# Local attention in blocks of 64 queries and 192 keys, and part of a gelu on GpSimd, in a Trainium2 decoder layer

## The chip, the core and the metric

The kernel runs on one core of a Trainium2 chip. Its engines each follow a fixed row of instructions of their own: TensorE (PE, with its weight loads shown as PEld), VectorE (DVE), ScalarE (ACT), GpSimd (POOL) and SyncE (SP), which issues most DMAs. An engine passes from one instruction to the next when the semaphores it waits for are reached, so an instruction that waits holds up all that stand behind it in the row of its engine. The metric is the device time of one execution in microseconds (us), median over runs; lower is better. One profiled execution gives the trace.

## The reference

One layer of a hybrid decoder on a prompt of 1024 tokens and eight single-token samples, width 1024, in fp32. Cut to what matters here:

```python
z = x @ w_in
xr, yr, q, k, v, xq, g = jnp.split(z, SPLIT_IDX, axis=-1)
xc, conv_new = causal_conv(xr, conv_buf, conv_w, conv_b)
hs, h_new = rg_lru(xc, h0, lru_wa, lru_ba, lru_wx, lru_bx, lru_lambda)   # h_t = a_t * h_(t-1) + u_t
a_out = hs * jax.nn.gelu(yr, approximate=True)        # branch a
s_out = swa_prompt(q, k, v, sinks)                    # branch s: 16 q heads, 4 kv heads of 64, window 128
c_out = mem_attn(xq, mem_k, mem_v)                    # branch c
merged = sum(gates[:, :, n] * (br @ w_branch[n]) for n, br in enumerate((a_out, s_out, c_out)))
h = layer_norm(ALPHA * x + merged @ w_out, ln1_g, ln1_b)
h = layer_norm(ALPHA * h + (jax.nn.silu(h @ w_gate) * (h @ w_up)) @ w_down, ln2_g, ln2_b)

# swa_prompt, per block of 128 queries: 256 keys, of which the band lets each query see 128
s = jnp.einsum('bnqkgd,bnmkd->bnkgqm', qb, kband) * scale
p = sink_softmax(jnp.where((m <= qi + 128) & (m > qi), s, -1e30), sinks)
o = jnp.einsum('bnkgqm,bnmkd->bnqkgd', p, vband)
```

## The kernel before

Every fp32 product is split in a high and a low part, and three matmuls (high by high, high by low, low by high) add up in one PSUM bank. ScalarE casts the high part and VectorE subtracts to get the low one (`split`). The stages follow one another: the projections (`project`), the attention to the memory, the local attention (`windows`), the rest of the branches, the output product and the feed-forward part. Names in the trace are those of the tiles.

*Projections.* 28 units of two column blocks of `w_in` (`UNITS`) go through seven steps each (`fast_step`, a Strassen scheme; 24 matmuls of 258 columns a step, in two halves p). The bank `ub` is built up in steps 0, 2, 4 and 6, and ScalarE copies it away after steps 0 and 2 (`p1s`, `u2s`), so step 4 has to wait for `u2s`; after step 6 `zb` is read from it. After each step, `pump` lets a side job go one stretch further. One kind of side job is `lru(m)` for m = 0 to 7: gates with a tanh, a square root, a scan along time on VectorE (`sq`), then the gelu of `yr`: a square, the product (g + 1) * yr, a tanh, once more (g + 1) * yr, and the product with the scan. `spill` writes q, k and xq, split in two, to DRAM (`scr_q`, ...).

*Windows.* For each of 4 kv heads and 8 blocks `b` of 128 queries: `win_scores` multiplies the four q heads of the group with 256 keys (128 in the first block). Queries and keys lie as high part over low part, 64 rows each, so two matmuls make one head's scores. A VectorE reduction adds the mask and finds the maximum, ScalarE takes the exponential with a running sum, and the four scalings by the reciprocal go to ScalarE (two), GpSimd and VectorE. `win_turn` transposes the probabilities by TensorE in two banks `bt` and splits them (`bph`, `bpl`); `win_values` multiplies them with `v` (bank `bo`). Values are stored as high and low parts side by side, so the two halves of the bank are added on the way out. Between blocks `fill(1)` puts one branch product of 24 matmuls (`bra`, `brc`: 8 tiles of weights, 3 matmuls each); `product` multiplies it by its gate and adds it into `M`. `windows` is a pipeline: scores of block b, a branch product, values of block b - 2, transposes of block b - 1.

What sets the order: a scheduler orders each engine's row when the kernel is built, by the program's order, dependences and its own estimates; `issue_after` pins an instruction behind another. `self.mark`, set in `mm3`, is such a pin: the values stand behind that matmul of the branch product.

## Time and profile before

| what | us |
|---|---|
| median of 3 runs | 1907.53 |
| lowest and highest | 1904.34 and 1908.17 |
| the profiled execution | 1903.72 |
| its span in the trace | 1902.0 |
| projections | 20 to 647 |
| attention to the memory | 647 to 816 |
| windows | 816 to 1012 |
| from there to the end | 1012 to 1902 |

The stages are read from the trace by their first and last matmuls, rounded. Rows of a timeline give start, duration, engine, line, operation and operands; x8 means that eight like rows are drawn together. Matmuls are pipelined: each is shown longer than the distance between two starts, and it is this distance that a matmul costs.

### The profile page before, as it was taken

How to read it: one execution, taken by the hardware profiler on the slowest of the kernel's cores; microseconds unless marked ns; L12 is line 12 of the kernel's file. 1: busy time of each engine (PE TensorE's matmuls, PEld its weight loads, DVE VectorE, ACT ScalarE, POOL GpSimd, SP SyncE). 2: the span in 40 equal slices, each digit the busy share in tenths (PEclk: the TensorE clock that was granted, in tenths of full speed). 3: DMA queues.
4: the chain of work that ended last, by engine and by line, in shares of the span. 5: the costliest groups of instructions: out<-in, count | busy, mean ns of one | idle time of the engine just before them, and what ended most of it. 6: DMA issues, size and time to landing. Idle time of an engine off the chain costs nothing.

```text
span 1902.0 us, 38091 instructions
## 1 busy us (share of the span) xinstructions
PE 1878.7 (99%) x14224; PEld 1860.1 (98%) x14224; DVE 1393.8 (73%) x2948; ACT 1018.4 (54%) x2187; POOL 288.4 (15%) x475
## 2 busy tenths in 40 slices
PE   8999999999999999999999999999999999999997
PEld 8999999999999999999999999999999999999997
DVE  8568877877887655469887667996766776686784
ACT  5455565555566555468775244653333333455574
POOL 1003000010000301012222111112111121222211
PEclk9999999999999999999999999999999999999999
DMA  7344444445345786577635563224353443586674
GB/s 233 111 147 167 142 165 152 141 158 198 120 163 184 256 268 197 161 191 216 166 110 164 178 213 112 90 91 162 132 166 123 144 156 128 185 295 219 202 230 133
DMA packets 177850, 321.98 MB, mean 169 GB/s; under 512 B 24577, under 2 KB 79953, under 8 KB 177665
## 3 DMA queue, kind: packets, MB, share of 16 engines
q1 hardware_dynamic: 157344, 258.90, 42.7%
q0 software_dynamic: 20320, 60.66, 9.6%
q8 instruction: 111, 1.82, 0.4%
q14 instruction: 75, 0.61, 0.1%
HBM read 234.50 MB, written 87.04 MB: 169 GB/s over the span
## 4 chain that ended last, share of the span: by engine, by line
PE 92%; ACT 3%; DVE 2%; DMA 1%; issue 1%; POOL 0%; SPq 0%; ACTq 0%; DVEq 0%; POOLq 0%
PE ub L338 5%; PE ub L337 5%; PE ub L339 5%; PE fb L1280 4%; PE fb L1281 4%; PE fb L1279 4%; PE dl L1567 3%; PE dl L1569 3%; PE dl L1568 3%; PE ud L338 3%; PE ud L339 3%; PE ud L337 3%; PE fd L1281 2%; PE fd L1280 2%; PE fd L1279 2%; PE op L134 2%
## 5 line engine op out<-in xcount | busy, mean ns | idle before, releaser
L641 ACT ACTIVATE bp<-bp,bst 128x257 f32<-128x257 f32 (+1 forms) x128 | 62.2, 488 | 30.0 <-DVE bst L637 29.9
L1343 POOL DMA_DIRECT2D scr_w<-dw x64 | 34.8, 544 | 271.0 <-DVE dw L1338 193.6
L97 ACT CAST u_1h<-us 128x512 fp32r<-128x512 f32 x48 | 29.8, 620 | 80.4 <-issue 45.2
L97 ACT CAST u_2h<-us 128x512 fp32r<-128x512 f32 x48 | 29.7, 619 | 78.6 <-PE fb L1280 37.8
L98 DVE TENSOR_TENSOR u_6l<-ur,u_6h 128x512 fp32r<-128x512 f32 x48 | 33.1, 690 | 46.7 <-PE fb L1281 28.4
L321 DVE TENSOR_TENSOR us<-ur,ur 128x512 f32<-128x512 f32 x96 | 65.9, 686 | 1.7
L321 DVE TENSOR_TENSOR us<-us,ur 128x512 f32<-128x512 f32 x96 | 65.9, 687 | 1.5
L134 PE MATMUL brs<-bsL,wbs_h 128*128 128x384 f32 (+2 forms) x192 | 61.3, 320 | 1.3 <-DVE bsL L98 1.3
L133 PE MATMUL brs<-bsH,wbs_h 128*128 128x258 f32 (+2 forms) x192 | 60.9, 320 | 0.3 <-ACT bsH L97 0.3
L135 PE MATMUL brs<-bsH,wbs_l 128*128 128x384 f32 (+2 forms) x192 | 61.1, 319 | 0.0
L833 POOL TENSOR_SCALAR tr<-th 128x1032 f32<-128x1032 f32 x8 | 12.0, 1496 | 315.1 <-DVE sq L832 110.9
L637 DVE CUSTOM_DVE_ANT_0 bp<-bs,mask,nsnk 128x256 f32<-128x256 f32 (+1 forms) x128 | 53.3, 459 | 4.9 <-PE bs L634 4.3
L97 ACT CAST u_4h<-us 128x512 fp32r<-128x512 f32 x48 | 29.8, 621 | 43.8 <-PE fb L1280 22.0
L97 ACT CAST u_0h<-ur 128x512 fp32r<-128x512 f32 x48 | 29.9, 622 | 42.7 <-PE ub L338 17.9
L648 POOL TENSOR_SCALAR bp<-bp,bst 128x256 f32<-128x256 f32 (+1 forms) x32 | 32.7, 1021 | 126.3 <-DVE bst L642 114.3
L97 ACT CAST u_3h<-ur 128x512 fp32r<-128x512 f32 x48 | 29.7, 620 | 41.0 <-PE ud L338 37.4
L98 DVE TENSOR_TENSOR u_5l<-us,u_5h 128x512 fp32r<-128x512 f32 x48 | 33.1, 689 | 21.9 <-PE ud L339 11.0
L805 POOL COPY pconv<-za 128x3 f32<-128x3 f32 x8 | 19.1, 2388 | 191.8 <-DVE za L369 189.2
L98 DVE TENSOR_TENSOR u_4l<-us,u_4h 128x512 fp32r<-128x512 f32 x48 | 33.0, 688 | 19.6 <-PE ub L339 10.9
L364 DVE TENSOR_TENSOR za<-uc,p1s 128x258 f32<-128x258 f32 x56 | 23.3, 421 | 31.6 <-PE uc L339 30.2
L1331 POOL DMA_DIRECT2D dw<-wdn x64 | 34.6, 540 | 77.8 <-DVE h_3l L98 45.7
L1307 ACT ACTIVATE ft<-za 128x516 f32<-128x516 f32 x40 | 25.3, 636 | 38.3 <-DVE za L1306 38.3
(1812 smaller groups left out, 8886.6 us busy)
## 6 DMA issues: line engine op xcount, KB each, us to landing
ur<-win SPq DMA_DIRECT2D x112, 256.0 KB, 2.9
ur<-wgu SPq DMA_DIRECT2D x80, 256.0 KB, 2.9
scr_f<-ft SPq DMA_DIRECT2D x40, 258.0 KB, 2.1
...
```

What stands on the lines that cost most here:

```text
L97: self.last_cast = ins = self.nc.scalar.copy(hi, src).ins
L98: self.last_sub = self.nc.vector.tensor_sub(lo, src, hi.bitcast(F32)).ins
L134: nc.tensor.matmul(ps, sh, ml, start=False, stop=False)
L135: self.last_mm = nc.tensor.matmul(ps, sl, mh, start=False, stop=closes and i == last).ins
L321: nc.vector.tensor_add(src, a, b)
L337: mm(sh[:, w], xh, start=opens and k == 0, stop=False)
L338: mm(sh[:, w], xl, start=False, stop=False)
L339: self.last_mm = mm(sl[:, w], xh, start=False, stop=k == 3).ins
L641: nc.scalar.activation(x, x, AF.Exp, bias=st[:, g:g + 1], scale=-1.0, accum_out=st[:, 4 + g:5 + g])
L1279: mm(sh[:, w], xh, start=opens and k == 0, stop=False)
L1280: mm(sh[:, w], xl, start=False, stop=False)
L1281: self.last_mm = mm(sl[:, w], xh, start=False, stop=k == 3).ins
```

## The change

In the windows, a block's 128 queries become two halves of 64. A tile of queries now holds 64 queries of two heads, and each half needs 192 keys only: eight matmuls of 192 columns for the scores, where there were eight of 256. The first and last 64 of the 256 keys concern one half each. They share a bank `be` of two transposes; the inner keys take four transposes in `bt`: six transposes instead of eight. `bt` is split as before (one cast, one subtraction of 512 columns), then the two ends are cast (both casts first) and subtracted, in tiles `bpe0` and `bpe1` that carry high part and low part over each other. The values are six matmuls of 256 columns instead of four of 512, and the end ones need `vd`, a copy of `v` with 64 rows twice, which eight more DMAs a kv head load. The reductions of the second pair of heads are pinned behind the last end subtraction. `scr_q` holds q in the new order, so that `spill` writes it in four DMAs with runs of 64 numbers instead of two with runs of 1024.

In the gelu, both products (g + 1) * yr leave VectorE for GpSimd, as an addition and a multiplication each. In `product`, the addition into `M` goes to GpSimd for the second branch (`c`), m below 6. The pin `mark` moves from the third to the last but one weight tile of a product.

```diff
+WK = 192
...
     def mm3(self, ps, terms, closes=True):
...
-            if i == 2:
+            if i == len(terms) - 2:
                 self.mark = self.last_mm
...
     def spill(self, z, m, name, scale):
...
-        nc.sync.dma_start(self.scr[name][:, m, 0, :], hp)
-        nc.sync.dma_start(self.scr[name][:, m, 1, :], zp)
+        for e, a in enumerate((hp, zp)):
+            if name == "q":
+                to = self.scr[name][:, m, e, :].rearrange("d (n u q) -> d u n q", u=2, q=64)
+                for u in range(2):
+                    nc.sync.dma_start(to[:, u], a[u * 64:(u + 1) * 64].rearrange("d (n q) -> d n q", q=64))
+            else:
+                nc.sync.dma_start(self.scr[name][:, m, e, :], a)
     def win_load(self, kv):
...
-        for g in range(4):
-            st = ph.tile([P, TP], F32R, tag="st", name=f"st{kv}_{g}", bufs=6)
+        q = [ph.tile([P, TP], F32R, tag="st", name=f"st{kv}_{n}", bufs=6) for n in range(4)]
+        for n in range(4):
             for e in range(2):
-                nc.sync.dma_start(st[e * 64:(e + 1) * 64].bitcast(F32), self.scr["q"][rows(g), 2 * kv + g // 2, e, :])
-            q.append(st)
+                nc.sync.dma_start(q[n][e * 64:(e + 1) * 64].bitcast(F32),
+                                  self.scr["q"][:, 2 * kv + n % 2, e, (n // 2) * TP:(n // 2 + 1) * TP])
         vs = ph.tile([P, 8, P], F32R, tag="vs", name=f"vs{kv}", bufs=2)
-        nc.sync.dma_start(vs.bitcast(F32), self.scr["v"][:, :, kv * P:(kv + 1) * P])
-        return ks, q, vs
+        v = self.scr["v"][:, :, kv * P:(kv + 1) * P]
+        nc.sync.dma_start(vs.bitcast(F32), v)
+        vd = [ph.tile([P, 4, 2, P], F32R, tag="vd", name=f"vd{kv}_{x}", bufs=2) for x in range(2)]
+        for x in range(2):
+            for r in range(2):
+                for e in range(2):
+                    nc.sync.dma_start(vd[x][e * 64:(e + 1) * 64, :, r, :].bitcast(F32),
+                                      v[r * 64:(r + 1) * 64, 4 * x:4 * x + 4])
+        return ks, q, (vs, vd)

     def win_scores(self, kv, ops, b):
...
-        p = self.ph.tile([P, 4, 257], F32, tag="p", name=f"bp{kv}_{b}", bufs=3)
-        pg = [p[:, g, :n] for g in range(4)]
-        nc.gpsimd.tensor_copy(p[:, :, n], snk)
+        p = self.ph.tile([P, 2, 2 * WK + 2], F32, tag="p", name=f"bp{kv}_{b}", bufs=3)
+        width = (WK, WK) if b else (64, P)
+        at = [(WK + 1 - width[0], WK + 1), (2 * WK + 1 - width[1], 2 * WK + 1)]
+        front, last = at[0][0] - 1, 2 * WK + 1
+        nc.gpsimd.tensor_copy(p[:, :, front:last + 1:last - front], snk.rearrange("p (r s) -> p r s", s=2))
+        pg = [p[:, pr, slice(*at[s])] for pr in range(2) for s in range(2)]
         for pr in range(2):
-            s = self.bank("s", f"bs{kv}_{b}_{pr}")
-            for u in range(2):
-                qq = q[2 * pr + u][:, b * P:(b + 1) * P]
-                o = s[:, u * 256:u * 256 + n]
-                nc.tensor.matmul(o, qq, ks[0][:, k0:k0 + n], start=True, stop=False)
-                nc.tensor.matmul(o, qq, ks[1][:, k0:k0 + n], start=False, stop=True)
-            for u in range(2):
-                g = 2 * pr + u
-                nc.vector.tensor_tensor_reduce(pg[g], s[:, u * 256:u * 256 + n], msk, 1.0, snk[:, g:g + 1],
-                                               ALU.add, ALU.min, st[:, g:g + 1])
+            ps = self.bank("s", f"bs{kv}_{b}_{pr}")
+            o = [ps[:, s * WK:s * WK + width[s]] for s in range(2)]
+            for s in range(2):
+                t0 = b * P + s * 64
+                qq = q[2 * (b // 4) + pr][:, 2 * t0 % TP:2 * t0 % TP + P]
+                kk = slice(t0 + 64 - width[s], t0 + 64)
+                nc.tensor.matmul(o[s], qq, ks[0][:, kk], start=True, stop=False)
+                nc.tensor.matmul(o[s], qq, ks[1][:, kk], start=False, stop=True)
+            for s in range(2):
+                g = 2 * pr + s
+                with self.tc.issue_after(self.last_sub) if pr else ExitStack():
+                    nc.vector.tensor_tensor_reduce(pg[g], o[s], self.mask[:, WK - width[s]:], 1.0, snk[:, g:g + 1],
+                                                   ALU.add, ALU.min, st[:, g:g + 1])
         for g in range(4):
-            x = p[:, g, :n + 1]
+            (k0, k1), s = at[g % 2], g % 2
+            x = p[:, g // 2, k0 - (s == 0):k1 + (s == 1)]
             nc.scalar.activation(x, x, AF.Exp, bias=st[:, g:g + 1], scale=-1.0, accum_out=st[:, 4 + g:5 + g])
...
-    def win_turn(self, kv, ops, b, pg):
+        return p
+
+    def win_turn(self, kv, ops, b, p):
         nc = self.nc
-        out = []
-        for kk in range(2 if b else 1):
-            pt = self.bank("t", f"bt{kv}_{b}_{kk}")
-            for g in range(4):
-                nc.tensor.transpose(pt[:, g * P:(g + 1) * P], pg[g][:, kk * P:(kk + 1) * P], self.ident)
-            hi = self.ph.tile([P, 512], F32R, tag="pt", name=f"bph{kv}_{b}_{kk}", bufs=4)
-            lo = self.ph.tile([P, 512], F32R, tag="pt", name=f"bpl{kv}_{b}_{kk}", bufs=4)
-            self.split(hi, lo, pt)
-            out.append((hi, lo))
-        return kv, ops[2], b, out
+        pt, pe = (self.bank("t", f"b{x}{kv}_{b}") for x in ("t", "e"))
+        nk = P if b else 64
+        for s in range(0 if b else 1, 2):
+            for pr in range(2):
+                o = s * 256 + pr * P
+                k0 = 2 * WK + 1 - P if s else 1
+                nc.tensor.transpose(pt[:, o:o + P], p[:, pr, k0:k0 + P], self.ident)
+        for pr in range(2):
+            nc.tensor.transpose(pe[:nk, pr * P:(pr + 1) * P], p[:, pr, P + 1:P + 1 + nk], self.ident)
+        hi = self.ph.tile([P, 512], F32R, tag="pt", name=f"bph{kv}_{b}", bufs=2)
+        lo = self.ph.tile([P, 512], F32R, tag="pt", name=f"bpl{kv}_{b}", bufs=2)
+        ends = [self.ph.tile([P, 256], F32R, tag=f"pe{s}", name=f"bpe{s}{kv}_{b}", bufs=1) for s in range(2)]
+        cols = slice(0 if b else 256, 512)
+        self.split(hi[:, cols], lo[:, cols], pt[:, cols])
+        own = [slice(s * 64, s * 64 + 64) for s in range(2)]
+        for s in range(2 if b else 1):
+            self.last_cast = nc.scalar.copy(ends[s][own[s]], pe[own[s], :256]).ins
+        for s in range(2 if b else 1):
+            self.last_sub = nc.vector.tensor_sub(ends[s][own[1 - s]], pe[own[s], :256],
+                                                 ends[s][own[s]].bitcast(F32)).ins
+        return kv, ops[2], b, (hi, lo, ends)
     def win_values(self, kv, vs, b, pp):
         nc = self.nc
         ov = self.bank("o", f"bo{kv}_{b}")
+        (v, vd), (hi, lo, ends) = vs, pp
         with self.tc.issue_after(self.mark):
-            for kk, (hi, lo) in enumerate(pp):
-                v = vs[:, max(b - 1, 0) + kk, :]
-                nc.tensor.matmul(ov, v, hi, start=kk == 0, stop=False)
-                nc.tensor.matmul(ov, v, lo, start=False, stop=kk == len(pp) - 1)
+            for s in range(2):
+                cols = slice(s * 256, s * 256 + 256)
+                terms = [(v[:, b - 1 + s, :], x[:, cols]) for x in (hi, lo)] if b or s else []
+                if b or not s:
+                    terms.append((vd[(b - s) // 4][:, (b - s) % 4, s, :], ends[s]))
+                for i, (x, y) in enumerate(terms):
+                    nc.tensor.matmul(ov[:, cols], x, y, start=i == 0, stop=i == len(terms) - 1)
         ob = self.ph.tile([64, 512], F32, tag="ob", name=f"bob{kv}_{b}", bufs=2)
-        nc.scalar.copy(ob, ov[64:128, :])
-        nc.vector.tensor_add(ob, ov[0:64, :], ob)
...
     def product(self, step, br, m, c, wb, gate):
...
-        nc.vector.tensor_add(dst, dst, t)
+        (nc.gpsimd if step == 1 and m < KT - 2 else nc.vector).tensor_add(dst, dst, t)
...
     def lru(self, m, xr, yr):
...
         nc.scalar.activation(g, yr, AF.Square, scale=GELU_A)
         yield
-        stt(g, g, 1.0, yr, op0=ALU.add, op1=ALU.mult)
+        nc.gpsimd.tensor_scalar(g, g, 1.0, None, op0=ALU.add)
+        nc.gpsimd.tensor_mul(g, g, yr)
         nc.scalar.activation(g, g, AF.Tanh, scale=GELU_C)
         yield
-        stt(g, g, 1.0, yr, op0=ALU.add, op1=ALU.mult)
+        nc.gpsimd.tensor_scalar(g, g, 1.0, None, op0=ALU.add)
+        nc.gpsimd.tensor_mul(g, g, yr)
         yield
...
-                  "q": [P, KT, 2, TP], "k": [P, 2, 2, TP], "v": [P, 8, 512]}
+                  "q": [64, KT, 2, 2 * TP], "k": [P, 2, 2, TP], "v": [P, 8, 512]}
...
-    q, m = np.arange(P)[:, None], np.arange(256)[None, :]
+    q, m = np.arange(P)[:, None] % 64, np.arange(WK)[None, :]
```

How the engines' rows change, at three places. Names carry the kernel's own numbers: `bt0_1` is kv head 0, block 1.

TensorE at the start of the windows, before: `bs` are scores, `bt` transposes, `bra` the branch product.

```order
L658 MATMUL bt0_0_0_11174<-ident_63,bp0_0_11097 128x128
L135 MATMUL bra6_0_11495<-H0_3h_8941,wba60_l_11486 128x384
L658 MATMUL bt0_0_0_11174<-ident_63,bp0_0_11097 128x128 x3
L633 MATMUL bs0_3_0_11278<-ks0_0_11010,st0_0_11016 128x256
L634 MATMUL bs0_3_0_11278<-ks0_1_11011,st0_0_11016 128x256
L633 MATMUL bs0_3_0_11278<-ks0_0_11010,st0_1_11019 128x256
L634 MATMUL bs0_3_0_11278<-ks0_1_11011,st0_1_11019 128x256
L133 MATMUL bra6_0_11495<-H0_4h_8939,wba61_h_11491 128x384
L658 MATMUL bt0_1_0_11257<-ident_63,bp0_1_11123 128x128 x3
L633 MATMUL bs0_3_1_11285<-ks0_0_11010,st0_2_11022 128x256
L658 MATMUL bt0_1_0_11257<-ident_63,bp0_1_11123 128x128
L634 MATMUL bs0_3_1_11285<-ks0_1_11011,st0_2_11022 128x256
```

TensorE at the same place, after.

```order
L675 MATMUL bt0_0_11216<-ident_63,bp0_0_11139 128x128 x2
L677 MATMUL be0_0_11217<-ident_63,bp0_0_11139 64x128 x2
L646 MATMUL bs0_2_0_11233<-ks0_0_11042,st0_0_11048 128x192
L647 MATMUL bs0_2_0_11233<-ks0_1_11043,st0_0_11048 128x192
L646 MATMUL bs0_2_0_11233<-ks0_0_11042,st0_0_11048 128x192
L647 MATMUL bs0_2_0_11233<-ks0_1_11043,st0_0_11048 128x192
L646 MATMUL bs0_2_1_11240<-ks0_0_11042,st0_1_11049 128x192
L647 MATMUL bs0_2_1_11240<-ks0_1_11043,st0_1_11049 128x192
L646 MATMUL bs0_2_1_11240<-ks0_0_11042,st0_1_11049 128x192
L647 MATMUL bs0_2_1_11240<-ks0_1_11043,st0_1_11049 128x192
L675 MATMUL bt0_1_11305<-ident_63,bp0_1_11165 128x128 x4
L677 MATMUL be0_1_11306<-ident_63,bp0_1_11165 128x128 x2
```

The transposes of blocks 0 and 1, which stood between matmuls of branch products, now follow with only the scores of block 2 between them.

ScalarE in step 2 of unit 20, beside the gelu of m = 5 (`ge5`), before: `p5s` and `u2s` are the copies of banks, `u20_6h` and the like the casts of weights.

```order
L362 COPY p5s20_0_6742<-ud20_0_6729 128x258
L97 CAST u20_6h_6800<-ur20_11_6433 128x512
L362 COPY p5s20_1_6757<-ud20_1_6744 128x258
L362 COPY u2s20_0_6782<-ub20_0_6680 128x258
L97 CAST u21_0h_6836<-ur21_00_6715 128x512
L362 COPY u2s20_1_6796<-ub20_1_6695 128x258
L97 CAST u21_1h_6878<-us21_1_6876 128x512
L847 ACT_TABLE_LOAD
L847 ACTIVATE ge5_6798<-ge5_6798 128x1032
L862 COPY drow_c6_6870<-drt_c6_6871 8x256
```

ScalarE there, after.

```order
L363 COPY p5s20_0_6760<-ud20_0_6747 128x258
L98 CAST u20_6h_6818<-ur20_11_6451 128x512
L363 COPY p5s20_1_6775<-ud20_1_6762 128x258
L880 ACT_TABLE_LOAD
L880 ACTIVATE ge5_6816<-ge5_6816 128x1032
L363 COPY u2s20_0_6800<-ub20_0_6698 128x258
L363 COPY u2s20_1_6814<-ub20_1_6713 128x258
L98 CAST u21_0h_6856<-ur21_00_6733 128x512
L98 CAST u21_1h_6898<-us21_1_6896 128x512
```

The table load and the tanh of `ge5` now stand ahead of `u2s20_0`; before they stood behind both copies and two casts.

ScalarE around unit 16, m = 4, before: `hi_q1` is the cast of a spill, `sq4` the square root that the scan of m = 4 needs.

```order
L436 ACTIVATE hi_q1_5456<-zb15_5342 128x1024
L362 COPY p5s16_1_5549<-ud16_1_5536 128x258
L829 ACT_TABLE_LOAD
L829 ACTIVATE sq4_5462<-th4_5407 128x1032
L362 COPY u2s16_0_5570<-ub16_0_5469 128x258
L362 COPY u2s16_1_5584<-ub16_1_5484 128x258
L97 CAST u17_0h_5636<-ur17_00_5507 128x512
L97 CAST u17_1h_5676<-us17_1_5674 128x512
L844 ACTIVATE ge4_5632<-zb13_4762 128x1032
L97 CAST u17_2h_5710<-us17_2_5708 128x512
```

ScalarE there, after.

```order
L363 COPY u2s16_0_5582<-ub16_0_5481 128x258
L98 CAST u17_0h_5649<-ur17_00_5519 128x512
L363 COPY u2s16_1_5596<-ub16_1_5496 128x258
L437 ACTIVATE hi_q1_5466<-zb15_5350 128x1024
L98 CAST u17_1h_5690<-us17_1_5688 128x512
L98 CAST u17_2h_5724<-us17_2_5722 128x512
L861 ACT_TABLE_LOAD
L861 ACTIVATE sq4_5474<-th4_5415 128x1032
L98 CAST u17_3h_5765<-ur17_01_5521 128x512
```

`hi_q1` and, behind it, the root `sq4` now stand behind `u2s16_1` and the casts of the next unit's weights, up to `u17_2h`.

18 lines of the change are left out of this document (8 added, 10 removed).

## The prediction

> **What bounds the kernel.** I read the page first: busy shares, then the chain that ended last.
>
> ```profile
> PE 1878.7 (99%) x14224; PEld 1860.1 (98%) x14224; DVE 1393.8 (73%) x2948; ACT 1018.4 (54%) x2187; POOL 288.4 (15%) x475
> ...
> PE 92%; ACT 3%; DVE 2%; DMA 1%; issue 1%; POOL 0%; SPq 0%; ACTq 0%; DVEq 0%; POOLq 0%
> ```
>
> TensorE is busy for 1878.7 of 1902.0 us and is 92% of the chain. So the change is worth what it takes out of TensorE's own row, less whatever it makes TensorE wait. Next, what TensorE waits for today (us in total, times, longest), and how full each engine is in the two stages that are edited, the projections (20 to 647 us) and the windows (816 to 1012 us):
>
> ```profile
> PE uo L133 <- ACT t00h L97: 5.0, 1, 5.0
> PE ub L337 <- DVE zb L366: 2.8, 1, 2.8
> PE brs L134 <- DVE bsL L98: 1.3, 1, 1.3
> ```
>
> ```profile
> 20.00:647.00 627.00, 623.67 (x5142) 622.54 (x5142) 487.47 (x954) 356.80 (x673) 57.91 (x64) 1.00 0.47 157
> ...
> 816.00:1012.00 196.00, 195.59 (x1295) 185.88 (x1294) 164.69 (x498) 156.26 (x447) 40.87 (x62) 1.00 0.57 157
> ```
>
> The numbers behind each window are its length and the busy us of PE, PEld, DVE, ACT and POOL. In both stages TensorE is idle for under 1%, with VectorE at 78% and 84%. Work taken from VectorE therefore buys nothing by itself: TensorE does not wait for it, apart from the one wait of 2.8 us.
>
> **Part 1, fewer and narrower products in the windows.** The timeline of one settled block before the change (start, us, instruction):
>
> ```profile
> 1003.94 0.40 PE L671 MATMUL bo<-bph,vs 128*128 128x512 f32 x1
> ...
> 1004.88 1.04 PE L658 MATMUL bt<-ident,bp 128*128 128x128 f32 x8
> ...
> 1005.99 0.28 PE L633 MATMUL bs<-ks,st 128*128 128x256 f32 x1
> ...
> 1006.59 0.28 PE L634 MATMUL bs<-ks,st 128*128 128x256 f32 x1
> 1006.71 0.34 PE L133 MATMUL brc<-H_0h,wbc_h 128*128 128x390 f32 x1
> 1006.88 0.34 PE L134 MATMUL brc<-H_0l,wbc_h 128*128 128x390 f32 x1
> ```
>
> Matmuls overlap, so the spacing of starts counts. The whole block takes 1006.71 - 1003.94 = 2.77 us: four 512-column value products in 0.94 us (0.235 each), eight scores of 256 columns at (1006.59 - 1005.99)/5 = 0.12, which is 0.96, and the remaining 0.87 for eight transposes (0.109 each). What does a product of 192 columns cost? The trace has none. The nearest narrower ones are the 128-column scores of a first block, whose weight loads start thus:
>
> ```profile
> 822.78 0.19 PEld L634 LDWEIGHTS bs<-ks,st 128*128 128x128 f32 x1
> 822.89 0.19 PEld L633 LDWEIGHTS bs<-ks,st 128*128 128x128 f32 x1
> ```
>
> They are 0.11 apart although half as wide as the others: below 256 columns the load of the next weights sets the pace. So 192 columns lie between 0.11 and 0.12; I take 0.11, because the 0.12 of 256 is already just above it. The Trainium skill ("TensorE: Matmul & The Clock Gate") gives a matmul as its columns over 2.4 GHz, some 82 ns for 192, but a load of 128 rows as about 107 ns; by the first figure alone the scores would save another 6 us, and the sum would be -8.3 instead of -2.3. The row of 0.11 agrees with the load.
>
> The new block has eight scores (0.88), six transposes (0.65) and six value products of 256 columns at 0.12 (0.72): 2.25, 0.52 less. There are 4 x 7 such blocks: 14.6 us. The four first blocks exchange two 512-wide value products (0.47) for three 256-wide ones (0.36): 0.4. Together **-15.0 us**, with ends at -12.5 (scores stay at 0.12) and -15.5.
>
> The casts, subtractions and masks that become smaller or move lie on VectorE and ScalarE beside TensorE in the settled period (one branch product of 24 matmuls to each block), and cost nothing there. If that cover were gone, the period would be VectorE's: 164.69 us of 196 before, and 18 `M` additions and the width of the reductions go off it. The 32 extra loads of `vd` are issued with the other loads half a group ahead, with 0.57 of DMA in use.
>
> **Part 2, the start of the windows.** Here the order changes against TensorE. Before, branch products stand between the scores and transposes of the first blocks; after, blocks 0 to 2 run with hardly any between. What the softmax takes: an exponential (from the page, mean 488 ns at 257 columns, so about 0.4 at 193), and block 0 before:
>
> ```profile
> L641 ACT ACTIVATE bp<-bp,bst 128x257 f32<-128x257 f32 (+1 forms) x128 | 62.2, 488 | 30.0 <-DVE bst L637 29.9
> ```
>
> ```profile
> 825.87 0.28 PE L634 MATMUL bs<-ks,st 128*128 128x128 f32 x1
> ...
> 827.95 0.17 DVE L642 RECIPROCAL bst<-bst 128x4 f32<-128x4 f32 x1
> ...
> 828.76 0.68 ACT L646 ACTIVATE bp<-bp,bst 128x128 f32<-128x128 f32 x2
> ...
> 829.02 0.27 PE L658 MATMUL bt<-ident,bp 128*128 128x128 f32 x1
> ```
>
> From the last score's end (about 826.0) to the first transpose are 3.0 us. In the new row only block 1's eight scores (0.9) lie in this gap, so TensorE waits about 2.0. Block 1: after the reciprocal of block 0, ScalarE has two scalings (0.6), four exponentials (about 0.4 each), and block 1's reciprocal and scaling (1.1) follow: 3.3 us. TensorE has 1.07 until block 0's transposes and 1.3 of work (block 0's four transposes, eight scores): 1.0 of waiting. The values of block 1 need a cast, a subtraction and two end pairs (about 2 us), behind four exponentials of block 2 (1.6 to 2); eight scores, three values and ten branch matmuls at 1006.88 - 1006.71 = 0.17 (3.0 us) cover most of it: 1.0 left. With 0.5 for the last end, **+4.5 us**. Ends: +1.7 (only the first, with a shorter queue on VectorE) and +7.0 (the second and third wait 2 us each).
>
> **Part 3, the gelu on GpSimd.** What it takes off VectorE (16 products of 1.22 us) was not waited for. What it adds to the chain of the tanh is a GpSimd multiplication of 1032 columns, which the trace does not have. Its neighbours, grouped by form (busy, mean ns):
>
> ```profile
> L648 POOL TENSOR_SCALAR bp<-bp,bst 128x256 f32<-128x256 f32 x28 | 29.2, 1042 | 86.6 <-DVE bst L642 74.6 <-PE bs L634 7.0 <-PE bt L658 4.9
> ...
> L833 POOL TENSOR_SCALAR tr<-th 128x1032 f32<-128x1032 f32 x8 | 12.0, 1496 | 315.1 <-DVE sq L832 110.9 <-ACT zb L1745 56.6 <-issue 53.8
> ...
> L1109 POOL TENSOR_TENSOR ls<-ls,lsq 128x264 f32<-128x264 f32 x6 | 4.7, 779 | 45.8 <-ACT ls L1101 32.9 <-ACT lsq L1101 12.7
> ```
>
> With the growth of the first two, (1.50 - 1.04)/776 per column, 1032 columns of two tensors cost 0.78 + 0.45 = 1.2 us; in proportion to the columns, 3.0. The ends are equally far in kind, so I take the middle, 2.1. In the new row of ScalarE, the tanh stands ahead of the copy `u2s_0` for m = 5, 6 and 7, where it stood behind it. The times of m = 5 before:
>
> ```profile
> 494.37 0.28 PE L337 MATMUL ub<-ts40h,u_4h 128*128 128x258 f32 x1
> ```
>
> ```profile
> 488.16 2.28 DVE L837 TENSOR_TENSOR_SCAN sq<-tr,ti 128x1024 f32<-128x1024 f32 x1
> ```
>
> ```profile
> 490.27 0.38 ACT L362 COPY u2s<-ub 128x258 f32<-128x258 f32 x1 [0.67 <-PE ub L339]
> ...
> 496.43 1.07 ACT L847 ACTIVATE ge<-ge 128x1032 f32<-128x1032 f32 x1
> ```
>
> ```profile
> 490.50 0.65 POOL L840 COPY pho<-sq 128x1 f32<-128x1 f32 x1 [4.64 <-DVE sq L838]
> 491.24 0.59 POOL L841 COPY sho<-sq 128x8 f32<-128x8 f32 x1
> ```
>
> TensorE opens step 4 of this unit at 494.37 and needs `u2s_0` by then. In the new GpSimd row the multiplication stands behind the two copies, so it starts at 491.83 and ends at 493.9; tanh until 495.0, copy until 495.4: 1.0 us of waiting. The same chain gives about 1.0 for m = 6 and 7; for m = 0 to 3, where tanh passes fewer of the copies, I put 0.7 in all: **+3.7**. Ends: at 1.2 us a multiplication the waits vanish (0); at 3.0 each of the three is 1.9, and the others 2: +8.
>
> **Part 4, m = 4.** The q units' spills are now four DMAs in runs of 256 bytes (1024 a DMA) instead of two in rows of 4096, and ScalarE's `hi_q` and the square root `sq4` have moved behind `u2s_1` and `u17_2h`. This is the place of the one wait of 2.8 us. VectorE and ScalarE before:
>
> ```profile
> 404.79 1.23 DVE L832 SCALAR_TENSOR_TENSOR sq<-tr,sq 128x1032 f32<-128x1032 f32 x1
> ...
> 410.71 1.23 DVE L846 SCALAR_TENSOR_TENSOR ge<-ge,zb 128x1032 f32<-128x1032 f32 x1
> ...
> 411.93 0.69 DVE L98 TENSOR_TENSOR u_0l<-ur,u_0h 128x512 fp32r<-128x512 f32 x1
> 412.53 0.42 DVE L366 SCALAR_TENSOR_TENSOR zb<-ub,p5s 128x258 f32<-128x258 f32 x1
> ```
>
> ```profile
> 405.44 1.07 ACT L844 ACTIVATE ge<-zb 128x1032 f32<-128x1032 f32 x1 [0.33 <-DMA scr_q<-zb]
> 406.91 0.62 ACT L97 CAST u_2h<-us 128x512 fp32r<-128x512 f32 x1 [0.40 <-PE ub L338]
> 407.55 1.28 ACT L847 ACT_TABLE_LOAD   x1
> ```
>
> Behind `u17_2h` (until 407.5) come a table load (1.28) and the root (1.07, as the other activations of this width): the step at 404.79 now starts at 409.9, 5.1 later. The scan and `zb` (412.53) follow in the same row, but no longer behind 1.23 + 0.69 of other work: 3.2 later, and `zb` is what TensorE waits for. With tanh now ahead of the next unit's `zb` copy (1.0 to 1.9 by the chain of part 3), **+4.5**; ends 0 (the spill lands and the root is early) and +7.5. The square of the gelu already waited 0.33 for a spill, so slower spills show here first. Elsewhere they are nearly a stage ahead of their readers.
>
> **The rest.** `M` additions on GpSimd (18 of 24 in the second branch): off the path, nothing; GpSimd is 79% idle in that stage, and no row waits for `M` until the third branch. The later `mark` only lets the values stand later in a branch product: counted in part 2.
>
> **The sum.** -15.0 + 4.5 + 3.7 + 4.5 = -2.3 us on the profiled execution's 1903.72: 1901.4. That execution is 3.8 us below the median of 1907.53; on the median it is **1905 us**.
>
> **Rivals.**
> - *The waits are hidden.* For it: the page's waits are few, and a wait early in a stage can be made up where TensorE's row has slack. Against: TensorE's row is fixed and has none. Parts 2 to 4 at about a third: -15 + 4, some 1896.5.
> - *GpSimd becomes the bound of the projections.* Place: the tanh ahead of `u2s_0`, `zb` and the weight casts in ScalarE's row. It decides from a multiplication of about 3 us on: then 8 + 7.5 + 4.5 against 15.0 is +5, 1912.5. For it: the widest TENSOR_SCALAR there already took 1.50 on the mean, and the same instruction 2.15 beside VectorE; against: one operand more need not triple it:
>
> ```profile
> 406.26 2.15 POOL L833 TENSOR_SCALAR tr<-th 128x1032 f32<-128x1032 f32 x1 [55.56 <-DVE sq L832]
> ```
>
> - *Scores run at their columns' cost*, against the row of 0.11: 0.12 x 192/256 = 0.09, another 8 x 0.02 x 28 = 4.5 us, 1900.5. By the figure of the Trainium skill quoted in part 1 it would be 6 us.
>
> **Chances.** The forecast 0.48, hidden waits 0.26, GpSimd 0.23, cheap scores 0.03. Within 0.2% (3.8 us of 1907.5, about what a measurement tells from no change) lie two thirds of the forecast's cases (its ends mix to -8 .. +3): 0.33; faster is 0.26 + 0.03 + 0.13 = 0.42; slower 0.23 and the rest of the forecast, 0.25. The range runs from 1895 (four fifths of the waits hidden) to 1914 (parts 3 and 4 near their upper ends); the forecast's own is 1899 to 1910.
>
> **What would show it.** Part 1: a settled block of 2.25 us from the first value product to the next branch product, and scores 0.11 apart. Part 2: waits of `bt` and `bo` on scalings and casts in the first 20 us of the windows. Part 3: waits of `ub` on `u2s` in units 20 to 27 and a GpSimd multiplication near 2.1 us. Part 4: the wait for `zb` grown from 2.8 to about 6. I am wrong if the multiplication is far from 2.1 us, or if VectorE, freed of 1.22 us twice a unit, moves the scan itself earlier.

## The result and the profile after

The changed kernel takes 1936.51 us (median, 1934.92 to 1938.13) against 1906.45 of the kernel before on the same chip: 1.6% slower, ratio 1.0159 with a 95% interval of 1.0145 to 1.0173. The prediction was 1905 us, with a range from 1895 to 1914: the sign and the size are both wrong. Busy shares and the chain of the page after:

```profile
PE 1881.6 (97%) x14228; PEld 1861.7 (96%) x14228; DVE 1398.2 (72%) x2946; ACT 1011.2 (52%) x2219; POOL 370.9 (19%) x525
...
PE 80%; DVE 7%; ACT 6%; POOL 3%; issue 3%; DMA 1%; SPq 0%; ACTq 0%; DVEq 0%; POOLq 0%
```

TensorE's share of the chain fell from 92 to 80%. The span grew by 32.2 us (1901.95 to 1934.13), and the first matmuls of the stages say where: the first `bra` starts 28.7 us later than before (650.1 to 678.8), so the projections lose 28.7; the attention to the memory loses 0.0, the windows 2.8, the rest 0.7. TensorE's waits (us in total, times, longest):

```profile
PE ub L338 <- ACT u2s L363: 9.7, 5, 3.1
PE ub L338 <- ACT zb L1781: 6.5, 4, 2.5
...
PE uc L338 <- DVE za L365: 4.2, 1, 4.2
PE ub L338 <- DVE zb L367: 1.8, 1, 1.8
PE bo L702 <- DVE bob L707: 1.6, 2, 1.3
```

The waits for `u2s`, `zb` (twice) and `za` belong to the projections, 22.2 us in all; before, only 2.8 and 0.5 us of `zb` were there. The delay against the kernel before, read where TensorE starts units 6, 9, 12, 15, 18, 21, 24 and 27, grows by 6.6 us at m = 0, then 3.4, 4.3 and 3.2 (17.4 for m = 0 to 3), 6.2 at m = 4, and 2.1, 2.1 and 1.9 for m = 5 to 7, 6.1 together (TensorE starts the projections 1.0 ahead). The prediction had 0.7, 4.5 and 3.0 for these three groups, and -15.0 + 4.5 = -10.5 for the windows, which became 2.8 longer.

The stretches of the projections and of the windows, in the columns of the prediction's table:

```profile
20.00:676.00 656.00, 630.71 (x5136) 625.94 (x5135) 496.34 (x935) 354.09 (x670) 129.48 (x95) 0.99 0.48 150
845.00:1043.00 198.00, 190.75 (x1289) 182.35 (x1288) 156.27 (x499) 147.57 (x467) 48.47 (x78) 0.99 0.65 176
```

In the windows VectorE and ScalarE are less busy than before (156.27 and 147.57, were 164.69 and 156.26), and TensorE, idle for 0.4 us of 196 before, is idle for 7 of 198: its work shrank, the time did not.

### The profile page after: what moved, and what is told of

Read it like the earlier page. It is cut to its first block, busy times and chain, and to the rows that moved or that the text cites. A ratio compares the mean times of both kernels' runs of the same rounds, so it can differ in the third digit from the quotient of the medians.

```text
span 1934.1 us, 38309 instructions
## 1 busy us (share of the span) xinstructions
PE 1881.6 (97%) x14228; PEld 1861.7 (96%) x14228; DVE 1398.2 (72%) x2946; ACT 1011.2 (52%) x2219; POOL 370.9 (19%) x525
## 4 chain that ended last, share of the span: by engine, by line
PE 80%; DVE 7%; ACT 6%; POOL 3%; issue 3%; DMA 1%; SPq 0%; ACTq 0%; DVEq 0%; POOLq 0%
PE ub L338 4%; PE ub L339 4%; PE fb L1314 4%; PE fb L1313 4%; PE fb L1315 4%; PE ub L340 4%; PE dl L1601 3%; PE dl L1603 3%; PE dl L1602 3%; PE ud L339 2%; PE ud L338 2%; PE fd L1315 2%; PE ud L340 2%; PE fd L1313 2%; PE fd L1314 2%
## 5 line engine op out<-in xcount | busy, mean ns | idle before, releaser
L656 ACT ACTIVATE bp<-bp,bst 128x193 f32<-128x193 f32 (+2 forms) x128 | 55.6, 436 | 45.7 <-DVE bst L651 45.6
L865 POOL TENSOR_SCALAR tr<-th 128x1032 f32<-128x1032 f32 x8 | 11.8, 1480 | 312.2 <-DVE sq L864 109.3
L322 DVE TENSOR_TENSOR us<-us,ur 128x512 f32<-128x512 f32 x96 | 70.2, 731 | 1.6
L99 DVE TENSOR_TENSOR u_6l<-ur,u_6h 128x512 fp32r<-128x512 f32 x48 | 33.1, 690 | 46.6 <-PE fb L1315 28.7
L663 POOL TENSOR_SCALAR bp<-bp,bst 128x192 f32<-128x192 f32 (+1 forms) x32 | 24.9, 778 | 155.1 <-DVE bst L657 150.0
L1365 POOL DMA_DIRECT2D dw<-wdn x64 | 34.6, 540 | 79.1 <-DVE h_3l L99 45.7
L651 DVE CUSTOM_DVE_ANT_0 bp<-bs,mask,nsnk 128x192 f32<-128x192 f32 (+2 forms) x128 | 44.7, 401 | 3.3 <-PE bs L647 2.3
L1603 PE MATMUL dl<-gh,wk 128*128 128x384 f32 x132 | 44.0, 335 | 0.0
L99 DVE TENSOR_TENSOR u_3l<-ur,u_3h 128x512 fp32r<-128x512 f32 x48 | 34.3, 715 | 11.8 <-PE ub L340 9.5
```

The costliest lines, as they stand in the source:

```text
L99: self.last_sub = self.nc.vector.tensor_sub(lo, src, hi.bitcast(F32)).ins
L322: nc.vector.tensor_add(src, a, b)
L1603: self.last_mm = mm(wl[:, w], xh, start=False, stop=k == KD - 1).ins
```

## What GpSimd does to the others

GpSimd's groups by form (busy, mean ns):

```profile
L878 POOL TENSOR_SCALAR ge<-ge 128x1032 f32<-128x1032 f32 x8 | 24.9, 3107 | 9.6 <-ACT ge L876 9.6
...
L879 POOL TENSOR_TENSOR ge<-ge,zb 128x1032 f32<-128x1032 f32 x8 | 21.9, 2736 | 0.3
L883 POOL TENSOR_TENSOR ge<-ge,zb 128x1032 f32<-128x1032 f32 x8 | 19.6, 2446 | 0.7
...
L865 POOL TENSOR_SCALAR tr<-th 128x1032 f32<-128x1032 f32 x8 | 11.8, 1480 | 312.2 <-DVE sq L864 109.3 <-ACT dcp L944 52.9 <-issue 50.7
```

The prediction priced the multiplication (2.1 us, ends 1.2 and 3.0; it took 2.4 to 2.7) and gave the addition ahead of it no time at all: its 2.1 us run from the end of the copies to the tanh. The addition is the longer of the two, 3.0 to 3.1 us on the mean. Nor would the nearest row have told this: L865, as wide, takes 1.5 us, but has two operations (times -1, plus 1) where the additions have one. A pair takes 5.4 to 5.8 us. Then the rows that wait for it, in the projections:

```profile
ACT ge L880 <- POOL ge L879: 30.9, 8, 5.4
...
ACT xch L98 <- DVE xc L834: 22.0, 7, 7.1
...
DVE ge L885 <- POOL ge L883: 19.0, 5, 5.2
```

ScalarE's tanh (L880) stands still for GpSimd's first pair, 30.9 us in eight waits; VectorE's last product of the gelu (L885) for the second pair, 19.0 us. Before, the tanh waited 9.5 us in five places for VectorE's product, the last product never, and the cast `xch` 6.0 us. Each wait holds the row behind it; what it costs depends on whether TensorE needs something from there (experiments 9 and 15). Here is the first case, m = 0: VectorE and ScalarE before, then the four engines after, each put in the order of time:

```profile
159.11 1.22 DVE L851 SCALAR_TENSOR_TENSOR ge<-sq,ge 128x1032 f32<-128x1032 f32 x1
166.71 1.26 DVE L802 SCALAR_TENSOR_TENSOR xc<-za,vec,xc 128x1021 f32<-128x1021 f32 x1
168.06 0.48 ACT L97 CAST xch<-xc 128x344 fp32r<-128x344 f32 x1 [2.30 <-DVE xc L802]
168.97 0.37 ACT L362 COPY u2s<-ub 128x258 f32<-128x258 f32 x1
```

```profile
154.16 2.79 POOL L879 TENSOR_TENSOR ge<-ge,zb 128x1032 f32<-128x1032 f32 x1
154.71 2.79 DVE L322 TENSOR_TENSOR us<-us,ur 128x512 f32<-128x512 f32 x1
156.98 1.07 ACT L880 ACTIVATE ge<-ge 128x1032 f32<-128x1032 f32 x1 [4.96 <-POOL ge L879]
161.56 2.42 POOL L883 TENSOR_TENSOR ge<-ge,zb 128x1032 f32<-128x1032 f32 x1
164.01 1.23 DVE L885 SCALAR_TENSOR_TENSOR ge<-sq,ge 128x1032 f32<-128x1032 f32 x1 [5.25 <-POOL ge L883]
172.22 1.27 DVE L834 SCALAR_TENSOR_TENSOR xc<-za,vec,xc 128x1021 f32<-128x1021 f32 x1
173.59 0.48 ACT L98 CAST xch<-xc 128x344 fp32r<-128x344 f32 x1 [7.12 <-DVE xc L834]
174.49 0.37 ACT L363 COPY u2s<-ub 128x258 f32<-128x258 f32 x1
174.91 0.39 PE L338 MATMUL ub<-ts41h,u_4h 128*128 128x258 f32 x1 [3.11 <-ACT u2s L363]
```

VectorE waits 5.25 us at L885; the convolution `xc` of the next m (L834) behind it is late; ScalarE's cast of `xc` waits 7.12 us; the copy `u2s` stands behind that cast, and TensorE's step 4 waits 3.11 us for `u2s`. The loss comes out three instructions and two engines away from GpSimd. The waits for ScalarE's `zb` come by the shorter way: ScalarE reads that bank behind the late tanh, and TensorE waits 1.35, 1.44, 2.48 and 1.24 us for it at m = 0 to 3.

The second row shows something else: a subtraction of 512 columns on VectorE, 0.68 us elsewhere, takes 2.79 us, and ends 0.55 us after GpSimd's multiplication. The clearest place is at m = 3:

```profile
361.19 2.47 POOL L879 TENSOR_TENSOR ge<-ge,zb 128x1032 f32<-128x1032 f32 x1
361.38 2.31 DVE L870 TENSOR_TENSOR sq<-tr,sh 128x8 f32<-128x8 f32 x1
...
434.64 0.13 DVE L870 TENSOR_TENSOR sq<-tr,sh 128x8 f32<-128x8 f32 x1
```

A product of 8 columns takes 2.31 us and ends with GpSimd's; the same line takes 0.13 us at m = 4, where no gelu step of GpSimd runs at that moment. Over the trace 100 VectorE rows overlap the 32 gelu steps. Together they are 26.4 us longer than the median of the same rows in the kernel before, nearly all of it in 19 rows that are longer by over 0.3 us. All 19 take both their operands from SBUF; none of the 29 rows that read a PSUM bank is longer. So VectorE, freed of 16 products of 1.22 us (19.5), was held up for more than that. The Trainium skill has the rule ("SBUF — State Buffer", Who interferes with whom): a VectorE instruction with two SBUF inputs contends with a GpSimd instruction that reads SBUF. These rows agree; the prediction did not weigh it.

## The experiments

Each is compared with the kernel before on the same chip. "Projections" and "windows" give by how many us the stage lengthened in the profiled run.

**1. The change without the gelu.** Both products back on VectorE; each time:

```diff
-        nc.gpsimd.tensor_scalar(g, g, 1.0, None, op0=ALU.add)
-        nc.gpsimd.tensor_mul(g, g, yr)
+        stt(g, g, 1.0, yr, op0=ALU.add, op1=ALU.mult)
```

> The changed kernel with both gelu products back on VectorE. Theory A (two rows stand still behind GpSimd: ScalarE's at the tanh L880, 30.9 us of waiting, and VectorE's at the last product L885, 19.0 us): the projections return to within 3 us of their length before, the whole is 1909 +- 3 us. Theory B (the new spill of q and the new rows around it hold up the projections by themselves): the projections stay 6 us or more longer, 1914 or above. The windows by both: 2 to 4 us longer than before, as in the changed kernel.

Measured: 1912.49 us, ratio 1.0039 (1.0027 to 1.0052). Projections +4.3, all of it at units 16 to 18 (m = 4); windows +3.1. So the gelu costs 23 us of the 30, each kernel taken against the kernel before on its own chip, and the rest of the change loses too.

**2. The gelu alone.** On the kernel before, each time:

```diff
-        stt(g, g, 1.0, yr, op0=ALU.add, op1=ALU.mult)
+        nc.gpsimd.tensor_scalar(g, g, 1.0, None, op0=ALU.add)
+        nc.gpsimd.tensor_mul(g, g, yr)
```

> The kernel before with only the gelu products moved to GpSimd in four steps. Theory A: the projections lose 22 to 29 us alone, 1929 to 1935 us. Theory B (much of the 28.7 us comes from the spill of q): under 15 us, below 1921.

Measured: 1934.97 us, 1.0157 (1.0143 to 1.0171). Projections +29.3, everything behind them +2.3. The loss needs neither the windows nor the new storage of q.

**3. The two-operation addition.** The whole change, with the addition as g * 1.0 + 1.0, both times.

```diff
-        nc.gpsimd.tensor_scalar(g, g, 1.0, None, op0=ALU.add)
+        nc.gpsimd.tensor_scalar(g, g, 1.0, 1.0, op0=ALU.mult, op1=ALU.add)
```

> The changed kernel with GpSimd's g + 1 written as g * 1.0 + 1.0 (two operations in one instruction, like the instruction L865, which took 1.37 us where this one took 2.84 without VectorE beside it). If the form with one operation is what costs: 1.4 us a step, each chain 1.5 us shorter, 16 of them on the path of ScalarE or VectorE, 8 to 20 us faster than the changed kernel. If the time hangs on something else (writing in place): 2.8 us again and no change.

GpSimd's groups by form:

```profile
L878 POOL TENSOR_SCALAR ge<-ge 128x1032 f32<-128x1032 f32 x8 | 10.6, 1320 | 9.6 <-ACT ge L876 9.6
L882 POOL TENSOR_SCALAR ge<-ge 128x1032 f32<-128x1032 f32 x8 | 9.5, 1187 | 5.7 <-ACT ge L880 5.7
```

Measured: 1925.01 us, 1.0108 (1.0086 to 1.0130). The same addition takes 1.3 us instead of 3.1, and the projections lose 15.3 instead of 28.7. The form of the addition is thus worth 13 us there and 10 in the median; with a pair of 4 us, nearer to the 3.0 that the prediction had as its upper end, the gelu still costs about 11 in the projections (15.3 less the 4.3 of experiment 1), where that end had 8.

**4. The windows and the new storage of q alone.** Experiment 1 with the `M` additions on VectorE and `mark` back at the third tile. Called W below.

```diff
-            if i == len(terms) - 2:
+            if i == 2:
...
-        (nc.gpsimd if step == 1 and m < KT - 2 else nc.vector).tensor_add(dst, dst, t)
+        nc.vector.tensor_add(dst, dst, t)
```

> The windows part alone: gelu and the additions into M on VectorE, the pin at the third tile as before. Theory A with the reading that VectorE bounds the middle of the windows (890 to 960 us): VectorE has 18 additions of 0.4 to 0.56 us more there, so 3 to 8 us slower than the same kernel with the additions on GpSimd, 1912 to 1917. If GpSimd's additions cost VectorE as much by standing beside it: the same, 1909.

Measured: 1911.25 us, 1.0031 (1.0020 to 1.0043). Projections +2.9, attention to the memory +1.5, windows +0.9, the rest +1.4. GpSimd's `M` additions brought nothing (1912.49 with them, intervals overlap).

**5. More cover at the start.** W, with a branch product behind the very first scores, and the transposes of the first blocks pinned behind the branch products ahead of them.

```diff
-                if last:
-                    fill(1)
+                fill(1)
...
-                turned = last and self.win_turn(*last)
+                with self.tc.issue_after(self.last_mm) if kv == 0 and b < 3 else ExitStack():
+                    turned = last and self.win_turn(*last)
```

> The windows part alone (as in the windows-only kernel, 1911.25 us) with one more branch product behind the first block's scores and the transposes of blocks 0 and 1 pinned behind the branch products that stand ahead of them in the program. If the start of the windows (waits of 0.35, 0.80, 1.20, 0.43 and 0.38 us between 825 and 836 us, and a half-clock stretch of 3.41 us behind them) is what eats the gain: these waits shrink to under 1.5 us and the half clock goes, 3 to 5 us faster. If the loss only moves (the products then lack later): the same.

Measured: 1912.24 us, 1.0032 (1.0021 to 1.0044): no gain. The waits of the start moved to one of 4.8 us for the weights of a branch product, `brc`, from ScalarE.

**6. The old storage of q.** W with `scr_q` and the spill as before; the loads then gather runs of 64 numbers.

```diff
-            if name == "q":
...
+            nc.sync.dma_start(self.scr[name][:, m, e, :], a)
...
-                nc.sync.dma_start(q[n][e * 64:(e + 1) * 64].bitcast(F32),
-                                  self.scr["q"][:, 2 * kv + n % 2, e, (n // 2) * TP:(n // 2 + 1) * TP])
+                to = q[n][e * 64:(e + 1) * 64].bitcast(F32).rearrange("d (n u q) -> d u n q", u=2, q=64)
+                for u in range(2):
+                    src = self.scr["q"][rows(u), 2 * kv + n % 2, e, (n // 2) * (TP // 2):(n // 2 + 1) * (TP // 2)]
+                    nc.sync.dma_start(to[:, u], src.rearrange("d (n q) -> d n q", q=64))
```

> The windows part alone with q stored as before (two DMAs of 4096-byte rows a spill) and read in runs of 256 bytes instead, 16 loads a kv head. If the spill of q and the rows it moved around unit 16 cost the 4 us at m = 4: the projections end within 1 us of before, and the whole is 3 to 5 us faster than the windows part alone, 1907. If the chain at m = 4 is late for another reason: the projections stay 3 us longer.

TensorE's waits:

```profile
PE bs L643 <- DVE bst L648: 7.0, 8, 2.2
PE bt L672 <- DVE bpl L99: 6.8, 4, 2.5
PE brc L134 <- ACT wbc_h L98: 5.4, 3, 5.0
...
PE ub L338 <- DVE zb L367: 2.8, 1, 2.8
```

Measured: 1944.47 us, 1.0202 (1.0187 to 1.0217). Projections +0.3, with the old 2.8 of `zb`: the loss at m = 4 is the spill's. But windows +37: in 64 loads of q beside the windows (32 in W) short runs cost far more than in the spills.

**7. Without the pin on the reductions.** W with the second pair's reductions free.

```diff
-                with self.tc.issue_after(self.last_sub) if pr else ExitStack():
+                with ExitStack():
```

> The windows part alone with the reductions of the second pair no longer pinned behind the last end subtraction. If the pin causes the waits of 0.2 us at the second pair's scores and the lost half of the gain in the settled blocks (6.7 us a period where 6.45 was expected): 3 to 5 us faster. If it protects the end subtractions, for which the values wait: the values wait more, the same or up to 4 us slower.

Measured: 1911.30 us, 1.0032 (1.0021 to 1.0043), W's 1911.25 within 0.1 us. No gain or loss from the pin can be measured.

**8 and 9. One pair of the gelu each.** The kernel before with only the first product, (g + 1) * yr ahead of the tanh, on GpSimd; then with only the second (the edit of experiment 2, once).

> The kernel before with only the first gelu product on GpSimd (addition and multiplication), the second on VectorE. By theory A the 29 us of both come from two rows that stand still: ScalarE's behind the tanh (waiting 30.9 us in eight places) and VectorE's behind the last product (19.0 in five). The first alone then costs 10 to 18 us, the second alone the rest. If only the tanh matters: 25 us or more here.

> The kernel before with only the second gelu product on GpSimd. The first alone cost 17.3 us in the projections, both 29.3. Theory A (two rows that stand still, one for each pair of steps): 12 us here by VectorE's wait for the last product, 8 to 16 allowed, 1914 to 1922. Rival (the tanh chain alone decides, and the second pair only adds behind it): under 4 us, below 1910.

Measured: the first 1923.74 us, 1.0094 (1.0079 to 1.0109), projections +17.3; the second 1911.65 us, 1.0039 (1.0023 to 1.0054), projections +5.3, which is less than expected. VectorE waits at the last product in the second:

```profile
DVE ge L852 <- POOL ge L850: 22.3, 8, 3.8
```

22.3 us of VectorE standing still cost 5.3 of the time; in the first, ScalarE's tanh waits 34.6 us and costs 17.3. Up to unit 15, which has m = 0 to 3, the first alone loses 8.3 and the second 6.3; the losses at m = 5 to 7 are the first's (7.3, the second 0.0). Alone they make 22.6, together 29.3 (experiment 2), as if each used up slack that the other needs; that is not shown.

**10. Half the spills of q from ScalarE's queue.** W, to free SyncE.

```diff
-                    nc.sync.dma_start(to[:, u], ...)
+                    (nc.sync, nc.scalar)[u].dma_start(to[:, u], ...)
```

> The windows part alone, with half of the DMAs of each q spill issued by ScalarE instead of SyncE, which puts the square root of m = 4 back ahead of the bank copies in ScalarE's row, while the runs of 256 bytes stay. If the row causes the loss at m = 4: the waits of 4.2 and 1.2 us there fall back to the 2.8 of before and the kernel is 3 to 5 us faster, 1907. If the runs of 256 bytes themselves are late: no gain, 1911.

ScalarE in unit 16, beside m = 4:

```profile
399.43 1.06 ACT L437 ACTIVATE hi_q<-zb 128x1024 fp32r<-128x1024 f32 x1 [5.05 <-DMA scr_q<-hi_q]
```

Measured: 1917.90 us, 1.0071 (1.0059 to 1.0084). Worse: ScalarE now waits 5.05 us for the spill itself, since the next cast writes the buffer that is still being read. The root of m = 4 does start earlier (403.77, in W 407.90), but the spills did not come out quicker: those that ScalarE issued landed in 6.7 to 8.5 us, where W's took 4.4 to 4.7 (medians). Before, 512 KB of `hi_q` in rows of 4096 bytes landed in 3.9 us; in W 256 KB in runs of 256 bytes take 4.4. That fits slow runs rather than a slow queue; it is not shown apart from the new order of the rows.

**11. One more scaling on ScalarE.** Experiment 10, with the first head's scaling moved from VectorE to ScalarE.

```diff
-            if g % 2:
+            if g % 2 or g == 0:
```

> As the kernel with half of the q spills on ScalarE, and also the scaling of the first head in the windows on ScalarE instead of VectorE (0.33 us a block). If VectorE bounds the stretch of 60 us in which branch c's rows are split: 2 to 4 us faster than without. If the order of the chain and not VectorE's load decides: the same, or slower where ScalarE's casts come later.

Measured: 1925.93 us, 1.0110 (1.0097 to 1.0124); windows +6.5, where experiment 10 has +1.4. More work on ScalarE costs at once there.

**12. Less work on VectorE in the windows.** W without the 24 subtractions that make the low parts of branch c's input.

```diff
+            if br == "c":
+                self.last_cast = self.row_cast = self.nc.scalar.copy(hi, lo.bitcast(F32)).ins
+                continue
```

> The windows part alone without the 24 subtractions that make the low parts of branch c's rows (the low part keeps the whole value, so the output is not the reference's): about 12 us less on VectorE between 870 and 935 us. If VectorE bounds that stretch: the 11 us lost there against an undisturbed row fall by half or more, 5 to 9 us faster than 1911. If not: under 2 us.

TensorE's waits:

```profile
PE bo L705 <- DVE bob L710: 1.4, 1, 1.4
PE bo L705 <- DVE bpe L690: 1.3, 1, 1.3
```

Measured: 1908.49 us, 1.0017 (1.0008 to 1.0026). The windows are 1.4 us shorter than in W, for some 12 us less on VectorE, and the waits stay: VectorE's amount of work does not set that stretch.

**13 and 14. One scaling less on ScalarE.** W with the fourth head's scaling on GpSimd, or the second head's on VectorE. The edit of 13; in 14 the condition is g == 3, and GpSimd keeps only g == 2.

```diff
-            if g % 2:
+            if g == 1:
```

> The windows' change alone (1911.2 us, ratio 1.0031), with one of ScalarE's two scalings of the probabilities in each block (the fourth head's) made by GpSimd. In the stretch 870 to 935 us ScalarE's row is dense: the cast of the transposes and the copy of the value bank stand behind exponentials, casts of H and of weights, and TensorE waits for what follows them (bo for bob, bo for bpe). If ScalarE's row is what bounds this stretch, 16 us less on it bring the windows 2 to 5 us back: 1906 to 1909, with waits for bob and bpe under 1 us in total each. If the waits are the length of the chain from scores to values, nothing changes or the slower scaling (1.0 us on GpSimd against 0.35 us on ScalarE) lengthens it: 1911 to 1914.

> The windows' change alone (1911.2 us, ratio 1.0031), with the other of ScalarE's two scalings (the second head's) made by VectorE. VectorE's load was shown not to bound the stretch 870 to 935 us (without 24 of its subtractions the waits stayed). If ScalarE's row does, the windows come 2 to 5 us back: 1906 to 1909. If the chain of one block does, 1910 to 1913, and the waits bo for bob and for bpe stay.

W from 870 to 935 us, then experiment 13 in the same stretch:

```profile
870.00:935.00 65.00, 61.35 (x406) 57.86 (x405) 56.43 (x174) 51.35 (x157) 10.36 (x20) 0.97 0.83 225
```

```profile
870.00:935.00 65.00, 60.55 (x404) 56.79 (x403) 56.04 (x175) 47.84 (x152) 18.74 (x27) 0.97 0.82 227
```

Measured: 13 takes 1910.8 us, 1.0022 (1.0012 to 1.0032), windows +0.3; 14 takes 1915.87 us, 1.0051 (1.0038 to 1.0064), windows +5.5. ScalarE lost 3.5 us of work in that stretch and TensorE did no more. So neither ScalarE's nor VectorE's amount of work bounds it by itself, while more work on either (11 and 14) costs at once; but 13 is no clean test, since GpSimd's scaling is slower (0.94 us on the mean, ScalarE's 0.45) and lengthens the chain. All this fits the chain of one block, from scores to values, passing back and forth between two nearly full rows; it is not shown which link decides.

**15 and 16. The same steps, waited for later.** Experiment 2 (15) and experiment 3 (16), with the tanh and the last product one stretch of the side job later than the pair each reads. GpSimd's steps are the same.

```diff
         nc.gpsimd.tensor_mul(g, g, yr)
+        yield
         nc.scalar.activation(g, g, AF.Tanh, scale=GELU_C)
...
         nc.gpsimd.tensor_mul(g, g, yr)
         yield
+        yield
         stt(g, sq, 0.5, g, op0=ALU.mult, op1=ALU.mult)
```

> The kernel before with both gelu products on GpSimd (1935.0 us, ratio 1.0157; projections +29.3 us), but with the tanh and the last product of the gelu one stretch of the side job later than the GpSimd pair they read, so that ScalarE's and VectorE's rows hold other work between: the tanh of ge3 stands twelve rows behind the square instead of two. GpSimd's four steps and their durations are the same. If the loss is rows standing still for GpSimd, the waits ge <- POOL (30.9 and 19.0 us in all) fall under 8 together and the projections lose under 6 us: 1906 to 1913. If GpSimd's work itself slows VectorE or TensorE, or is late whatever stands between, over 15 us stay: 1920 to 1935.

> The whole change, with the addition written in the two-operation form (g * 1.0 + 1.0, 1.3 us instead of 3.1) and the same later tanh and last product as in the run before. Only the windows' loss and m = 4 should be left, as with the change of the windows alone (1.0031) or with the gelu on VectorE (1.0039): 1908 to 1914. If GpSimd's work costs by contention even where nothing waits for it, 1916 to 1925.

In 15: waits of ScalarE and VectorE in the projections, TensorE's wait for `u2s`, and the stretch at the first branch product:

```profile
ACT ge L849 <- POOL ge L847: 27.1, 8, 6.0
...
ACT H_0h L97 <- DMA H_0l<-scr_a: 8.9, 2, 6.0
...
DVE ge L855 <- POOL ge L852: 3.8, 2, 2.5
```

```profile
PE ub L337 <- ACT u2s L362: 1.7, 2, 1.0
```

```profile
660.00:675.00 15.00, 11.73 (x36) 7.64 (x37) 8.06 (x16) 10.55 (x23) 7.51 (x14) 0.78 0.92 315
```

Measured: 15 takes 1921.27 us, 1.0083 (1.0067 to 1.0100; the profiled run is its slowest, 1926.85); 16 takes 1937.16 us, 1.0160 (1.0144 to 1.0176). By its time 15 lies in the second case, and 16 beyond both, but the stages say otherwise. When unit 18 starts, 15 is 5.2 us late where experiment 2 was 21.7, and 16 is 2.0 late where experiment 3 was 12.0. VectorE is held up by GpSimd no less than before (30.6 us over the rows in 15 and 37.3 in 16, counted as above), and ScalarE still waits 27.1 us at the tanh, but at places where TensorE does not need what is behind it. So the loss up to there is where the rows wait, not GpSimd's amount of work. The later stretches then make the last gelu late: in 16 units 18 to 27 lose 10.5, and in both the last product of the gelu starts only 2.7 us ahead of the first branch product (22 before, 21 in the change). So the first two branch products starve (TensorE is busy for 11.73 of 15 us) while ScalarE waits for the loads of branch a's input, 8.9 us in 15 and 5.9 in 16; 9.5 and 10.1 are lost there. The loss was put off, not removed.

No version beats the kernel before.

## Why the prediction was wrong

The miss has two parts. On the span, -2.3 us became +32.2. The gelu (m = 0 to 3 and 5 to 7) took 23.5 where 3.7 were predicted, 19.8 of the miss; the windows +2.8 where -10.5 were predicted, 13.3; m = 4 added 1.7 and the other stages take off 0.3.

**Part 1 held.** A settled block after the change:

```profile
1036.93 0.28 PE L702 MATMUL bo<-bph,vs 128*128 128x256 f32 x1
...
1037.65 0.60 PE L675 MATMUL bt<-ident,bp 128*128 128x128 f32 x4
...
1038.23 0.34 PE L646 MATMUL bs<-ks,st 128*128 128x192 f32 x1
...
1039.19 0.36 PE L134 MATMUL brc<-H_0h,wbc_h 128*128 128x390 f32 x1
```

It takes 1039.19 - 1036.93 = 2.26 us (predicted 2.25), with the scores 0.11 to 0.12 apart. Of the two figures of the Trainium skill that the prediction weighed ("TensorE: Matmul & The Clock Gate"), the load's of about 107 ns agrees, not the columns'. Priced by the median spacing of each kind of matmul in its own trace, all matmuls of the windows come to 13.0 us less in W than before, where 15.0 were predicted.

**Part 2 held at the start, and one of its covers failed later.** Up to 860 us W loses 5.5 us against these spacings (the kernel before 1.4; 4.5 predicted). The step that failed is "cost nothing there", said of the casts and subtractions in the settled period. From 870 to 935 us W loses another 9.7 us, where the kernel before loses 1.8 in the like stretch; 6.2 of them stand directly ahead of value products, which read what these casts and subtractions make (at 893 one waits 1.1 us for its bank instead). The prediction counted VectorE's work and found less; it did not follow one block's chain, which now has three casts and three subtractions between transposes and values, where there were two of each. Experiments 11 to 14 speak against the amount of work of one engine alone; the deciding link stays open. So the windows of W gave 13.0 and lost 13.9 more than before beyond the spacings: +0.9.

**Part 3 failed, and carries the larger part of the miss.** Two steps of it decide. First, the pair: "a GpSimd multiplication of 1032 columns" is not all that the chain gets, since each is preceded by an addition, 3.1 us, for which the sum has no term (experiment 3: 10 us for its form alone). Second, "for m = 0 to 3 ... I put 0.7 in all" was not worked out: it was 17.4. The chain was drawn for ScalarE's tanh and `u2s` alone; `zb`, read behind the same tanh, was not counted for m = 0 to 3, and the last product on VectorE, whose 5.25 us delay the next convolution, was named nowhere. Of VectorE the text says only that what was taken off it "was not waited for". Up to unit 15 both ways count: 8.3 us by the first pair alone and 6.3 by the second alone (experiments 8 and 9). A further point was missing but carries little by itself: GpSimd's reads held VectorE up for 26.4 us, and yet 15, with 30.6, was only 5.2 us late at unit 18. For m = 5 to 7 the mechanism was right and the size was off: 6.1 against 3.0, the price of a longer pair.

**Part 4 held in its place.** The root of m = 4, in the rows of ScalarE and VectorE, and the wait:

```profile
425.27 1.07 ACT L861 ACTIVATE sq<-th 128x1032 f32<-128x1032 f32 x1
...
428.17 1.22 DVE L864 SCALAR_TENSOR_TENSOR sq<-tr,sq 128x1032 f32<-128x1032 f32 x1
...
432.17 0.55 PE L338 MATMUL uc<-t10h,u_3h 128*128 128x258 f32 x1 [4.22 <-DVE za L365]
```

The step that was at 404.79 is at 428.17, 23.4 later, of which 16.5 had been lost earlier: 6.9 against 5.1 predicted. TensorE's wait falls on `za` (4.2) first, then `zb` (1.8). With 6.2 us in the change and 3.8 to 4.0 without the gelu on GpSimd (W and experiment 1, by the starts of units 15 and 18), 4.5 was a fair price; experiment 6 shows that the new storage of q causes it.

**The rest and the rivals.** The `M` additions brought nothing, as put. The rival "GpSimd becomes the bound" had the right side at 0.23, but its 1912.5 fell short for the same reasons: a pair of 5.6 us lies far beyond "a multiplication of about 3 us", and it too looked at ScalarE's row alone. Nor did GpSimd become the bound: it is busy for 19% of the span. What counts is when each of its steps ends.
